# A diffusion block on one core: the first adaLN steps in another order, and some q products among them

## The chip, the cores and the metric

The kernel runs on one core of a Trainium2 chip. Its time is the device time of one execution in microseconds (us); lower is better. The time before is the median of three runs. A profile is one execution taken by the hardware profiler; all durations below come from that one. Engines are called PE (TensorE matmul), PEld (TensorE weight load), DVE (VectorE), ACT (ScalarE), POOL (GpSimd) and SP (SyncE, which here only issues DMAs).

## The reference, cut to what matters

One layer of a diffusion block: 256 latent tokens `x` and 256 context tokens `ctx`, width 2048. The part that the change touches is the start:

```python
sh1, sc1, g1, sh2, sc2, g2 = adaln(c, w_ada, b_ada)              # silu(c) @ w_ada + b_ada, in six
h  = modulate(rms_norm(x, norm_mix_g), sh1, sc1)                 # x * (1 + scale) + shift
csh1, csc1, ... = adaln(c_ctx, w_ada, b_ada)
hc = modulate(rms_norm(ctx, norm_mix_g), csh1, csc1)
q, k, v = split(h @ w_qkv, 3);  _, kc, vc = split(hc @ w_qkv, 3)  # 16 heads of 128
...                                                               # attention, w_o, gated residual
x = x + g2 * conv_ffn(modulate(rms_norm(x, norm_ffn_g), sh2, sc2), ...)
```

Keys and values are needed of both streams, queries of the latent one alone. Everything is float32.

## The kernel before

Features lie on partitions: the 2048 features of a token are 16 blocks of 128, called kt = 0 to 15. Tokens 0 to 255 are the latent stream (`xl`), 256 to 511 the context (`xc`). A float32 product is made of three products of halves: `hh` and `hl` are high and low part of the modulated input, `wh` and `wl` those of a weight, and L372, L373 and L374 multiply hh by wh, hh by wl and hl by wh. Each is a matmul of 512 columns for one tile of 128 tokens and one block kt. A weight is split by a cast on ACT (L157, `wh`) and a subtraction on DVE (L158, `wl`); the loaded tiles (`wr`) have four buffers, `wh` three, `wl` two.

The first stage goes by grains (L46): block 0, block 1, then seven pairs of blocks. Shift and scale of a grain come from an adaLN step (`ada_step`, L391): four loads of `w_ada` (tiles `wx`, four buffers, each loaded by two DMAs for shift and scale), sixteen small matmuls against the 32-column tile `s32` (L407), a copy to SBUF on ACT (`ev`, L414), transposes on PE (L417), and five small DVE operations that give `shT` and `gsT` (L422 to L430). `modulate` (L436) then makes a DVE product in place (L441), `hh` on ACT (L446) and `hl` on DVE (L447) for each block and stream.

Before the first products of a stream its rms must be known. `stats` (L349) squares the input on ACT in eight pieces (L354), adds them up on DVE (L359), sums over partitions by matmuls with one column (L229), takes the root (POOL L197, DVE L198 to L202), and spreads the result by a matmul (L220) and a copy (L222).

`first_products` (L455) gives the products of a grain in six pieces, each for two of the four tiles of 128 tokens (the first two are latent, the last two context): the first 512 columns of k, which gather in four PSUM banks over the whole stage (`pj`), and twice 512 columns of v, each grain of which goes through two banks (`mx`) and is copied (L472, ACT, first grain) or added (L474, DVE) to `vsum`. The two `mx` banks are also those of the sums and of the spread root in `stats`: they are given out in the order of the program, and each user waits until the one before has been read.

The program begins with `x`, its stats and adaLN step 0, the split of two weights (`ahead`, L182), the load of `ctx`, the latent pieces of k and of the first v of grain 0, the stats of `ctx`, and its modulation. Then a loop goes over the grains: the pieces of grain j stand between the four parts of step j+1. All loads of inputs and weights are issued by SP, in one queue. The order within an engine is set when the program is built, by a planner that simulates the instructions in time and goes by program order where several are ready; `tc.issue_after(i)` puts an instruction behind i on the same engine, and `tc.high_priority()` puts it ahead in the planner's choice. `plan` (L166) lists all weight tiles in the order of use.

After this stage `project(0, 2)` (L681) makes the first 512 columns of q from all 16 blocks: 2 token tiles, 16 blocks and 3 halves, 96 matmuls. Then come attention, the output projection, and the FFN, which takes over half of the time.

Of the kernel before, what the change touches and what calls it, by code (L numbers as in the profile page):

```python
# [15 lines left out]
P = 128  # L16
# [36 lines left out]
def block_kernel(  # L53
# [93 lines left out]
    last, hold = [], []  # L147

    def wpair(src, k0, kn, c0, cn):

        w = wload(src, k0, kn, c0, cn)
        hi = wp.tile([P, KT, CH], F32R, tag="wh", name="wh", bufs=3)
        lo = wp.tile([P, KT, CH], F32R, tag="wl", name="wl", bufs=2)
        with ExitStack() as order:
            for ins in hold:
                order.enter_context(tc.issue_after(ins))
            a = nc.scalar.copy(hi[:, :kn, :cn], w[:, :kn, :cn])  # L157
# [9 lines left out]
    for kt, n in GRAINS:  # L167
        plan.extend((w_qkv, kt, n, c, CH) for c in (D, 2 * D, 2 * D + CH))
    for g, cols in ((0, (0,)), (1, (D, 0)), (2, (2 * D, D, 0)), (3, (D, 0, 2 * D))):
        for c in cols:  # L170
            plan.extend((w_qkv, kt, KT, c + g * CH, CH) for kt in range(0, KD, KT))
    for pieces in WO:
# [175 lines left out]

    def stats(xin, name):  # L349

        sacc = None
        for kt in range(0, KD, 2):
            sq = xp.tile([P, 2, T], F32, tag="sq", name="sq", bufs=3)
            nc.scalar.activation(sq, xin[:, kt : kt + 2, :], AF.Square)  # L354
# [7 lines left out]
        return rstd_rows(xp, sums, name, nc.vector.tensor_copy)  # L362

    def nat(psl, tt0, w, kt0, n, first, last):

        wh, wl = w
        for i, pt in enumerate(psl):
            ts = slice((tt0 + i) * P, (tt0 + i + 1) * P)
            for k in range(n):
                kt = kt0 + k  # L370
                a, z = first and k == 0, last and k == n - 1
                nc.tensor.matmul(pt, hh[:, kt, ts], wh[:, k, :], start=a, stop=False)  # L372
                nc.tensor.matmul(pt, hh[:, kt, ts], wl[:, k, :], start=False, stop=False)  # L373
                nc.tensor.matmul(pt, hl(kt, ts), wh[:, k, :], start=False, stop=z)  # L374
            side.tick(side.rate)
            ada.tick(ada.rate)

    def project(c0, nt):
        psl = [pj() for _ in range(nt)]
        ada.rate = ADA_RATE[nt]  # L380
        for kt in range(0, KD, KT):
            nat(psl, 0, weight(w_qkv, kt, KT, c0, CH), kt, KT, kt == 0, kt == KD - KT)
        ada.rate = 0.0
        return psl
# [5 lines left out]

    def ada_step(b0, nb, work=()):  # L391

        ap_ = ms()
        n = 2 * nb * P
        for q in range(4):
            if q < len(work):
                work[q]()
            w = xp.tile([P, 4 * CH], F32, tag="wx", name="wx", bufs=4)[:, : 4 * n]
# [7 lines left out]
            for k in range(4):  # L406
                nc.tensor.matmul(  # L407
                    ap_[32 * k : 32 * k + 32, :n], s32[:, 4 * q + k, :], w[:, k * n : (k + 1) * n],
                    start=(q == 0), stop=(q == 3), tile_position=(0, 32 * k),
                )  # L410
        for piece in work[4:]:
            piece()
        ev = xp.tile([P, CH], F32, tag="ev", name="ev")
        nc.scalar.copy(ev[:, :n], ap_[:, :n])  # L414
        sp = ms()
# [4 lines left out]
        for which, dst in ((0, shT), (1, gsT)):  # L420
# [12 lines left out]
            op0=ALU.add, op1=ALU.mult,  # L433
        )

    def modulate(b0, nb, streams=None):  # L436

        for st, x_ in streams or ((0, xl), (1, xc)):
            t = slice(st * T, (st + 1) * T)
            for kt in range(b0, b0 + nb):  # L440
                nc.vector.scalar_tensor_tensor(  # L441
                    out=x_[:, kt, :], in0=x_[:, kt, :], scalar=gsT[:, kt, st : st + 1], in1=rb[st],
                    op0=ALU.mult, op1=ALU.mult,
                )
                sh = shT[:, kt, st : st + 1]
                nc.scalar.activation(hh[:, kt, t], x_[:, kt, :], AF.Identity, bias=sh)  # L446
                nc.vector.scalar_tensor_tensor(  # L447
                    out=hl(kt, t), in0=x_[:, kt, :], scalar=sh, in1=hh[:, kt, t].bitcast(F32),
                    op0=ALU.add, op1=ALU.subtract,
                )  # L450


    vsums = [kv.tile([P, 4, CH], F32, tag=tag, name="vsum") for tag in ("qq", "kl")]

    def first_products(b0, nb):  # L455

        st = {}
# [5 lines left out]

        def v_pair(g, h0):
            acc, c0 = vsums[g], 2 * D + g * CH
            if h0 == 0:
# [8 lines left out]

        return [
            lambda: k_pair(0), lambda: v_pair(0, 0), lambda: k_pair(2),
            lambda: v_pair(0, 2), lambda: v_pair(1, 0), lambda: v_pair(1, 2),
        ]
# [193 lines left out]

    def out_of_psum(pts, dst):

        for tt, pt in enumerate(pts):
            nc.scalar.copy(dst[:, tt, :], pt)
# [277 lines left out]
```

## Time and profile before

| | us |
|---|---|
| median of three runs (1419.31 to 1419.57) | 1419.35 |
| the profiled execution, its own time | 1419.36 |
| span of its instructions in the profile | 1417.6 |
| PE busy / DVE busy / ACT busy | 1386.8 / 1022.4 / 694.9 |
| first product of x (L372) starts | 23.72 |
| first product of ctx (L372) starts | 35.79 |
| moved by DMA | 317.13 MB |

In a timeline a row is: start in us, length in us, engine, line, operation, output and inputs with their shapes, how many were merged (x8), and in brackets the idle time of the engine before it and what ended that. In a table of windows a row is: the window, its length, then busy time and instructions of PE, PEld, DVE, ACT and POOL, the granted TensorE clock (1.00 is full), the busy share of the 16 DMA engines and the GB/s moved. In the chain of waits a row is start, length, and what the end of the program hung on then.

### The profile page before, as it was taken

Reading aid. Unit: us, or ns where it says so; the run is one execution under the profiler, and the core shown is the slowest. Engines: PE = TensorE matmul, PEld = TensorE weight load, DVE = VectorE, ACT = ScalarE, POOL = GpSimd, SP = SyncE. Lnnn points to the kernel's source line nnn. Section 1 sums busy time; section 2 is a strip of 40 time slices with the busy share of each in tenths; the row PEclk is TensorE's granted clock in tenths of the full one; section 3 lists DMA queues with packets and bytes.
Section 4 is the critical chain, followed back from the end, with each engine's and each line's share of the span. In section 5 each row is a group of like instructions: output and inputs, shape, how many; then the busy total and the mean of one; then the engine's idle time right before and its main releaser. Section 6 shows DMA issues by size and latency. Waiting matters only on the chain.

```text
span 1417.6 us, 20783 instructions
## 1 busy us (share of the span) xinstructions
PE 1386.8 (98%) x7608; PEld 1164.8 (82%) x7608; DVE 1022.4 (72%) x1669; ACT 694.9 (49%) x1212; POOL 59.9 (4%) x64
## 2 busy tenths in 40 slices
PE   4999999999999999999899999999999999999998
PEld 2566788888888888888788888888888888888888
DVE  4555678878877888788777888778787675545454
ACT  4322254564454564554565655556555554333343
POOL 1000010020010020000100000000000000000000
PEclk9999999999999999999899999999999999999999
DMA  9999637768776869475667777777776666666554
GB/s 304 357 353 292 223 104 237 227 214 257 233 238 192 276 201 291 157 250 178 225 187 237 237 236 238 225 237 235 231 230 189 175 192 197 188 200 201 169 181 154
DMA packets 208918, 317.13 MB, mean 224 GB/s; under 512 B 23360, under 2 KB 87744, under 8 KB 208816
## 3 DMA queue, kind: packets, MB, share of 16 engines
q1 hardware_dynamic: 208688, 315.79, 71.5%
q8 instruction: 59, 0.97, 0.3%
q14 instruction: 43, 0.35, 0.1%
q10 hardware_dynamic: 128, 0.01, 0.0%
HBM read 312.75 MB, written 3.01 MB: 223 GB/s over the span
## 4 chain that ended last, share of the span: by engine, by line
PE 94%; DMA 2%; DVE 2%; SPq 1%; ACT 1%; issue 1%; POOL 0%; DVEq 0%; ACTq 0%; POOLq 0%
PE pj L723 20%; PE pj L729 10%; PE mx L723 10%; PE pj L372 8%; PE pj L373 8%; PE pj L374 8%; PE ms L723 7%; PE mx L729 5%; PE ms L729 4%; PE mx L372 2%; PE mx L373 2%; PE ms L407 2%; PE mx L374 2%; DMA wx<-in_w_ada 1%; PE ms L627 1%; SPq L401 1%
## 5 line engine op out<-in xcount | busy, mean ns | idle before, releaser
L158 DVE TENSOR_TENSOR wl<-wr,wh 128x1024 fp32r<-128x1024 f32 (+2 forms) x425 | 478.1, 1126 | 284.8 <-PE pj L729 102.3
L157 ACT CAST wh<-wr 128x1024 fp32r<-128x1024 f32 (+2 forms) x425 | 412.6, 972 | 535.3 <-PE pj L723 164.3
L373 PE MATMUL pj<-wl,hh 128*128 128x512 f32 x512 | 202.7, 396 | 0.0
L374 PE MATMUL pj<-wh,hl 128*128 128x512 f32 x512 | 200.1, 393 | 0.0
L372 PE MATMUL pj<-wh,hh 128*128 128x512 f32 x512 | 193.0, 396 | 2.5 <-ACT hh L446 2.5
L274 DVE SCALAR_TENSOR_TENSOR acc<-wa,sT,acc 128x512 f32<-128x512 f32 x240 | 183.2, 765 | 2.5
L723 PE MATMUL pj<-hf,wh 128*128 128x512 f32 x688 | 176.1, 395 | 2.0 <-DVE hf L815 2.0
L723 PEld LDWEIGHTS pj<-hf,wh 128*128 128x128 f32 x688 | 124.6, 190 | 25.1 <-DVE hf L815 2.8
L372 PEld LDWEIGHTS pj<-wh,hh 128*128 128x128 f32 x512 | 95.7, 188 | 26.4 <-issue 3.4
L373 PEld LDWEIGHTS pj<-wl,hh 128*128 128x128 f32 x512 | 96.5, 188 | 21.5 <-DVE wl L158 0.9
L374 PEld LDWEIGHTS pj<-wh,hl 128*128 128x128 f32 x512 | 96.5, 188 | 18.8
L729 PEld LDWEIGHTS pj<-hf,wl 128*128 128x128 f32 x688 | 93.7, 190 | 6.7
L723 PE MATMUL mx<-hf,wh 128*128 128x512 f32 x352 | 97.7, 394 | 0.0
L729 PE MATMUL pj<-hf,wl 128*128 128x256 f32 x688 | 96.9, 283 | 0.0
L723 PE MATMUL ms<-hf,wh 128*128 128x512 f32 x336 | 90.9, 390 | 0.0
L723 PEld LDWEIGHTS ms<-hf,wh 128*128 128x128 f32 x336 | 63.1, 188 | 14.2
L474 DVE TENSOR_TENSOR vsum<-vsum,mx 128x512 f32<-128x512 f32 x64 | 43.1, 682 | 34.3 <-PE mx L374 34.1
L723 PEld LDWEIGHTS mx<-hf,wh 128*128 128x128 f32 x352 | 60.6, 190 | 7.8
L729 PEld LDWEIGHTS mx<-hf,wl 128*128 128x128 f32 x352 | 53.7, 189 | 6.8
L729 PE MATMUL mx<-hf,wl 128*128 128x256 f32 x352 | 55.9, 282 | 0.0
L729 PE MATMUL ms<-hf,wl 128*128 128x256 f32 x336 | 54.7, 283 | 0.0
L407 PE MATMUL ms<-wx,s 128*32 128x512 f32 (+1 forms) x288 | 36.9, 582 | 16.3 <-DMA wx<-in_w_ada 16.3
(248 smaller groups left out, 2029.6 us busy)
## 6 DMA issues: line engine op xcount, KB each, us to landing
wr<-in_w_up SPq DMA_DIRECT2D x160, 512.0 KB, 4.2
wa<-in_w_ada SPq DMA_DIRECT2D x128, 512.0 KB, 4.8
wr<-in_w_qkv SPq DMA_DIRECT2D x93, 512.0 KB, 4.2
wr<-in_w_down SPq DMA_DIRECT2D x63, 512.0 KB, 4.6
wx<-in_w_ada SPq DMA_DIRECT2D x56, 512.0 KB, 8.6
wr<-in_w_o SPq DMA_DIRECT2D x24, 512.0 KB, 5.0
wr<-in_w_down SPq DMA_DIRECT2D x45, 256.0 KB, 3.1
wr<-in_w_up SPq DMA_DIRECT2D x16, 384.0 KB, 3.4
```

What stands on the lines that cost most here:

```text
L157: a = nc.scalar.copy(hi[:, :kn, :cn], w[:, :kn, :cn])
L158: b = nc.vector.tensor_tensor(out=lo[:, :kn, :cn], in0=w[:, :kn, :cn], in1=hi[:, :kn, :cn].bitcast(F32), op=ALU.subtract,)
L274: nc.vector.scalar_tensor_tensor(out=acc, in0=w[:, k, :], scalar=s, in1=acc, op0=ALU.mult, op1=ALU.add)
L372: nc.tensor.matmul(pt, hh[:, kt, ts], wh[:, k, :], start=a, stop=False)
L373: nc.tensor.matmul(pt, hh[:, kt, ts], wl[:, k, :], start=False, stop=False)
L374: nc.tensor.matmul(pt, hl(kt, ts), wh[:, k, :], start=False, stop=z)
L401: load = nc.sync.dma_start(w.rearrange("p (k s f) -> p k s f", k=4, s=2)[:, :, which, :], w_ada[q * CH : (q + 1) * CH, c0 : c0 + n // 2].r ...
L407: nc.tensor.matmul(ap_[32 * k : 32 * k + 32, :n], s32[:, 4 * q + k, :], w[:, k * n : (k + 1) * n], start=(q == 0), stop=(q == 3), tile_pos ...
L474: nc.vector.tensor_add(acc[:, h0 + i, :], acc[:, h0 + i, :], pr_[i])
L627: nc.tensor.transpose(tp[:, kt * P : (kt + 1) * P], pr[:, kt * P : (kt + 1) * P], ident)
L723: nc.tensor.matmul(pts[b][:, : t1 - t0], wh[:, k, bs], mov(kt, slice(t0, t1)), start=(kt == 0 and t0 == 0), stop=False,)
L729: nc.tensor.matmul(pts[b][:, :T], wl[:, k, bs], mov(kt, slice(0, T)), start=False, stop=(kt == kn - 1),)
```

## The change

The start of the program, up to adaLN step 3, is put in another order; no product is added or left out.

- Weights of q for blocks 0 and 1 are loaded early (`Q_EARLY`), and their products are made with grains 0 and 1 in the `mx` banks and gathered in `qsum` (ACT copies for block 0, DVE additions for block 1). `project(0, 2)` starts at block 2, and `qsum` is added when its banks are read, on DVE in place of a copy on ACT.
- The latent modulation of block 0 stands ahead of the splits of the first two weights (`hold`). The squares of `ctx` stand behind it, and the split of the third weight behind the last of these squares.
- The last two pairs of squares are no longer added up on DVE: they go into the sums as four more parts, 12 matmuls of one column and not 8.
- The four parts of an adaLN step are loaded together, ahead of the pieces; for steps 0 and 1, which are half as wide, two parts share a `wx` buffer. Before the loop there stand the load of the third weight and those of step 1.
- `BEHIND` says, for steps 1 to 3, how many pieces of the grain before stand ahead of each part of the step. For step 1 it is (2, 2, 2, 2): all of its matmuls come behind the context pieces of k and of the first v, and the last two pieces (both of the second v) behind the matmuls. Their rest (`ada_end`) and their modulation get priority.

```diff
+Q_EARLY = 2
+
+BEHIND = {0: (2, 2, 2, 2), 1: (2, 2, 4, 5), 2: (2, 2, 4, 4)}
...
     for kt, n in GRAINS:
-        plan.extend((w_qkv, kt, n, c, CH) for c in (D, 2 * D, 2 * D + CH))
+        cs = (0,) * (kt == 0) + (D, 2 * D, 2 * D + CH) + (0,) * (0 < kt < Q_EARLY)
+        plan.extend((w_qkv, kt, n, c, CH) for c in cs)
...
-    def stats(xin, name):
+    def squares(xin, behind=()):
...
+                for ins in behind:
+                    order.enter_context(tc.issue_after(ins))
+                square = nc.scalar.activation(sq, xin[:, kt : kt + 2, :], AF.Square)
             if sacc is None:
                 sacc = sq
-            else:
+            elif kt < KD - 4:
                 nacc = xp.tile([P, 2, T], F32, tag="sacc", name="sacc", bufs=2)
                 nc.vector.tensor_add(nacc, sacc, sq)
                 sacc = nacc
-        sums = col_sums(mx()[:, 0:2], (sacc[:, 0], sacc[:, 1]))
+            else:
+                parts.extend((sq[:, 0], sq[:, 1]))
...
+    def ada_step(ws, b0, nb, work=(), behind=None):
         ap_ = ms()
         n = 2 * nb * P
+        done = 0
+        for q, w in enumerate(ws):
+            with ExitStack() as order:
+                for piece in work[done : behind[q] if behind else q + 1]:
+                    piece()
+                    done += 1
+                if behind:
+                    order.enter_context(tc.issue_after(last_mm[0]))
+                for k in range(4):
+                    mm = nc.tensor.matmul(
...
+        with ExitStack() as order:
+            if behind:
+                order.enter_context(tc.issue_after(mm.ins))
+            for piece in work[done:]:
+                piece()
+        with ExitStack() as order:
+            if behind or not work:
+                order.enter_context(tc.high_priority())
+            return ada_end(ap_, b0, nb)
...
+        q = [lambda: pair(qsum, 0, 0)]
+        pieces = [
             lambda: k_pair(0), lambda: v_pair(0, 0), lambda: k_pair(2),
             lambda: v_pair(0, 2), lambda: v_pair(1, 0), lambda: v_pair(1, 2),
         ]
+        return (q if b0 == 0 else []) + pieces + (q if 0 < b0 < Q_EARLY else [])
 
     stream(xl, xT)
-    rb = [stats(xl, "x")[0]]
-    ada_step(*GRAINS[0])
+    rb = [stats(squares(xl)[0], "x")[0]]
+    copied = ada_step(ada_load(*GRAINS[0]), *GRAINS[0])
+    with tc.high_priority():
+        x_ins = modulate(*GRAINS[0], ((0, xl),))
+    hold[:] = [copied, x_ins[0]]
     ahead()
+    hold.clear()
     stream(xc, ctxT)
-    modulate(*GRAINS[0], ((0, xl),))
+    loaded.append(wload(*plan[0]))
+    tiles = ada_load(*GRAINS[1])
+    parts, square = squares(xc, x_ins[-1:])
+    hold[:] = [square]
     work = first_products(*GRAINS[0])
-    work[0]()
-    work[1]()
-    rb.append(stats(xc, "c")[0])
-    modulate(*GRAINS[0], ((1, xc),))
+    for piece in work[:3]:
+        piece()
+    hold.clear()
+    with tc.high_priority():
+        rb.append(stats(parts, "c")[0])
+        modulate(*GRAINS[0], ((1, xc),))
     for j, grain in enumerate(GRAINS):
-        work = first_products(*grain) if j else work[2:]
+        work = first_products(*grain) if j else work[3:]
         if j + 1 < len(GRAINS):
-            ada_step(*GRAINS[j + 1], work)
-            modulate(*GRAINS[j + 1])
+            if j:
+                tiles = ada_load(*GRAINS[j + 1])
+            ada_step(tiles, *GRAINS[j + 1], work, BEHIND.get(j))
+            with ExitStack() as order:
+                if j in BEHIND:
+                    order.enter_context(tc.high_priority())
+                modulate(*GRAINS[j + 1])
...
-    q = split_q(out_of_psum(project(0, 2), qw))
+    q = split_q(out_of_psum(project(0, 2, Q_EARLY), qw, qsum))
```

More of the change, by code (lines that the diff above doesn't have):

```diff
@@ L360, in stats @@
                 sacc = nacc
-        sums = col_sums(mx()[:, 0:2], (sacc[:, 0], sacc[:, 1]))
-        return rstd_rows(xp, sums, name, nc.vector.tensor_copy)
+            else:
+                parts.extend((sq[:, 0], sq[:, 1]))
+        return (sacc[:, 0], sacc[:, 1], *parts), square.ins
+    def stats(parts, name):
+        return rstd_rows(xp, col_sums(mx()[:, 0:2], parts), name, nc.vector.tensor_copy)
+    last_mm = []
     def nat(psl, tt0, w, kt0, n, first, last):
@@ L373, in nat, with project @@
                 nc.tensor.matmul(pt, hh[:, kt, ts], wl[:, k, :], start=False, stop=False)
-                nc.tensor.matmul(pt, hl(kt, ts), wh[:, k, :], start=False, stop=z)
+                mm = nc.tensor.matmul(pt, hl(kt, ts), wh[:, k, :], start=False, stop=z)
+                last_mm[:] = [mm.ins]
             side.tick(side.rate)
             ada.tick(ada.rate)
-    def project(c0, nt):
+    def project(c0, nt, k_lo=0):
         psl = [pj() for _ in range(nt)]
         ada.rate = ADA_RATE[nt]
-        for kt in range(0, KD, KT):
-            nat(psl, 0, weight(w_qkv, kt, KT, c0, CH), kt, KT, kt == 0, kt == KD - KT)
+        for kt in range(k_lo, KD, KT):
+            nat(psl, 0, weight(w_qkv, kt, KT, c0, CH), kt, KT, kt == k_lo, kt == KD - KT)
         ada.rate = 0.0
@@ L405, in ada_step, with ada_end @@
             loads.append(load.ins)
[L406 to L412, printed above, removed]
+            ws.append(w)
+        return ws
+    def ada_step(ws, b0, nb, work=(), behind=None):
+        ap_ = ms()
+        n = 2 * nb * P
+        done = 0
[8 more added lines that the diff above has]
+                    mm = nc.tensor.matmul(
+                        ap_[32 * k : 32 * k + 32, :n], s32[:, 4 * q + k, :],
+                        w[:, k * n : (k + 1) * n], start=(q == 0), stop=(q == 3),
+                        tile_position=(0, 32 * k),
+                    )
+        with ExitStack() as order:
[7 more added lines that the diff above has]
+            return ada_end(ap_, b0, nb)
+    def ada_end(ap_, b0, nb):
+        n = 2 * nb * P
         ev = xp.tile([P, CH], F32, tag="ev", name="ev")
-        nc.scalar.copy(ev[:, :n], ap_[:, :n])
+        copied = nc.scalar.copy(ev[:, :n], ap_[:, :n])
         sp = ms()
```

42 lines of the change are left out of this document (26 added, 16 removed).

## The prediction, made before the changed kernel was run

> **What bounds the kernel now.** I read the page first, then a table of windows, then the timeline of the first 60 us. From the page the busy times and the first line of the chain, from the windows the stretch behind the first context product and the next 100 us:
>
> ```profile
> PE 1386.8 (98%) x7608; PEld 1164.8 (82%) x7608; DVE 1022.4 (72%) x1669; ACT 694.9 (49%) x1212; POOL 59.9 (4%) x64
> ...
> PE 94%; DMA 2%; DVE 2%; SPq 1%; ACT 1%; issue 1%; POOL 0%; DVEq 0%; ACTq 0%; POOLq 0%
> ...
> 35.79:54.00 18.21, 17.48 (x92) 10.38 (x95) 9.42 (x24) 8.57 (x14) 0.00 (x0) 1.00 1.08 356
> 60.00:160.00 100.00, 100.00 (x515) 62.48 (x514) 56.74 (x113) 26.57 (x40) 0.00 (x0) 1.00 0.93 305
> ```
>
> TensorE sets the end. From the first context product at 35.79 on it has no hole but 0.73 us up to 54, and none at all from 60 to 160. So the change is worth what it does to two things: the moment from which PE is closed, and the PE work that still lies behind that moment. Work that moves from the closed part into the open part is a gain by its length; work that moves the other way is a loss.
>
> The open part first, up to the first product of x:
>
> ```profile
> 18.25 1.08 PE L407 MATMUL ms<-wx,s 128*32 128x256 f32 x8 [0.54 <-DMA wx<-in_w_ada]
> 18.85 1.33 ACT L157 CAST wh<-wr 128x512 fp32r<-128x512 f32 x2 [6.60 <-DMA wr<-in_w_qkv]
> 20.09 0.36 ACT L414 COPY ev<-ms 128x256 f32<-128x256 f32 x1
> ...
> 22.64 0.63 ACT L354 ACTIVATE sq<-xc 128x512 f32<-128x512 f32 x1 [0.37 <-DMA xc<-in_ctxT]
> 23.17 0.49 ACT L446 ACTIVATE hh<-xl,shT 128x256 fp32r<-128x256 f32 x1
> 23.72 0.80 PE L372 MATMUL pj<-wh,hh 128*128 128x512 f32 x1 [2.46 <-ACT hh L446]
> 24.31 0.63 PE L373 MATMUL pj<-wl,hh 128*128 128x512 f32 x1
> 24.74 0.63 PE L372 MATMUL pj<-wh,hh 128*128 128x512 f32 x1
> ```
>
> Step 0 ends on PE at 19.33 with its last load; its copy waits for the casts until 20.09, and `hh` stands behind a square until 23.17. Two matmuls lie 0.43 us apart here. Then the context:
>
> ```profile
> 25.59 1.15 ACT L354 ACTIVATE sq<-xc 128x512 f32<-128x512 f32 x2 [0.30 <-DMA xc<-in_ctxT]
> ...
> 28.46 1.07 ACT L472 COPY vsum<-mx 128x512 f32<-128x512 f32 x2 [1.21 <-PE mx L374]
> 28.86 0.64 PE L407 MATMUL ms<-wx,s 128*32 128x256 f32 x8 [0.21 <-DMA wx<-in_w_ada]
> 29.43 1.05 PE L229 MATMUL mx<-ones,sacc 128*128 128x1 f32 x8
> ...
> 32.09 0.42 DVE L215 TENSOR_TENSOR cd<-ident,cr 128x256 f32<-128x256 f32 x1
> 32.48 0.64 PE L407 MATMUL ms<-wx,s 128*32 128x256 f32 x8 [1.16 <-DMA wx<-in_w_ada]
> 33.05 0.70 PE L220 MATMUL mx<-cd,ones 128*128 128x256 f32 x2
> 33.78 0.42 DVE L222 COPY cb<-mx 128x256 f32<-128x256 f32 x1 [1.27 <-PE mx L220]
> 34.26 0.64 PE L407 MATMUL ms<-wx,s 128*32 128x256 f32 x8 [0.51 <-DMA wx<-in_w_ada]
> 34.95 0.37 ACT L414 COPY ev<-ms 128x256 f32<-128x256 f32 x1 [5.42 <-PE ms L407]
> 35.22 0.51 ACT L446 ACTIVATE hh<-xc,shT 128x256 fp32r<-128x256 f32 x1
> 35.38 0.44 PE L417 MATMUL ms<-ident,ev 128*128 128x128 f32 x2 [0.48 <-ACT ev L414]
> 35.79 0.50 PE L372 MATMUL pj<-wh,hh 128*128 128x512 f32 x1
> 37.44 0.51 ACT L446 ACTIVATE hh<-xl,shT 128x256 fp32r<-128x256 f32 x1 [1.70 <-DVE xl L441]
> ```
>
> The last of `ctx` has been squared at 26.74, but the sums start only at 29.43: their bank is one of the two `mx` banks that v of grain 0 holds until ACT has copied it. The wait behind the sums is used: all of step 1, four parts and the transposes, runs in it and is over when the context starts. That is the part of the old order which the change gives up.
>
> **The change, part by part.** The prices of PE work in the closed part:
>
> ```profile
> 43.73 0.39 PE L374 MATMUL mx<-wh,hl 128*128 128x512 f32 x1
> 44.05 1.06 PE L407 MATMUL ms<-wx,s 128*32 128x512 f32 x8
> 45.04 0.50 PE L372 MATMUL mx<-wh,hh 128*128 128x512 f32 x1
> 45.38 0.39 PE L373 MATMUL mx<-wl,hh 128*128 128x512 f32 x1
> ...
> 53.72 1.06 PE L407 MATMUL ms<-wx,s 128*32 128x512 f32 x8 [0.73 <-DMA wx<-in_w_ada]
> ...
> 171.07 0.39 PE L373 MATMUL pj<-wl,hh 128*128 128x512 f32 x1
> 173.33 0.39 PE L374 MATMUL mx<-wh,hl 128*128 128x512 f32 x1
> ```
>
> The second of the last two rows is the tenth matmul after the first: 2.26 / 10 = 0.226 us each. A part of adaLN between products costs 0.1 us more on the way in (44.05 - 43.73 - 0.23) and 0.1 on the way out (45.38 - 45.04 - 0.23).
>
> 1. *q products.* 12 matmuls (2 blocks, 2 tiles, 3 halves) leave the closed stage of `project`: -2.71 us. The 6 of block 0 go into the open part. The 6 of block 1 need step 1 and stay closed: +1.36. Net **-1.36**.
> 2. *Step 1 behind the context.* Its matmuls can't fill the wait any more. Four parts at 0.57 (29.43 - 28.86), transposes 0.41 (35.79 - 35.38) and one way in and out 0.2 become closed work: **+2.9**.
> 3. *Start of the context.* Without casts ahead of the copy and squares ahead of `hh`, step 0's end at 19.33 gives `hh` by about 22.3 (20.09 to 23.17 is 3.08, less 0.7 behind the square; 19.35 + 2.4 + its own 0.5). Only then come the eight squares of `ctx`, 0.575 each: to 26.9, no earlier than now. On ACT follow two copies of q out of `mx` (1.07) and the cast of the first v (0.66), which now stands behind the squares: 28.6. The latent v products start between 28.0 and 28.6, take 6 x 0.226, are copied (0.53), and the sums start between 29.5 and 30.5; 12 matmuls instead of 8, at 0.13, end between 31.1 and 32.1. From there to the first context product it was 30.48 to 35.79, 5.3 us; two delays go: L220 waited 0.5 behind a part of step 1 (32.51 to 33.05), `hh` 0.5 behind `ev`. 4.3 remain: 35.4 to 36.4. So the shorter chain on DVE, the priority and the free queue of PE are eaten up by q's six matmuls and copies ahead of the bank. I take **0**, ends -0.4 and +0.6.
> 4. *Wait at 53.72.* Three groups of work now stand ahead of that part, so the load is there: **-0.73**.
> 5. *Parts taken together.* Step 2 in three groups for four, step 3 in two: 3 x 0.2, **-0.6**.
> 6. *Start of grains 1 and 2.* From the end of step 1's last part (34.90) to the end of `hh` (37.95) it takes 3.05. The second v of grain 0, 12 matmuls, and the transposes cover 3.1: nothing. For step 2 as many matmuls are left (a pair of v, a pair of q), but two blocks are to be modulated and vsum additions stand on DVE: **+0.5**, ends 0 and 1.3.
> 7. *The clock.* This stall shows elsewhere in this trace, ahead of the FFN, with its windows:
>
> ```profile
> 676.68 0.64 PE L729 MATMUL ms<-om,wl 128*128 128x256 f32 x4
> 679.09 1.68 PE L229 MATMUL ms<-ones,sq 128*128 128x1 f32 x8
> 683.12 1.19 PE L220 MATMUL mx<-yd,ones 128*128 128x256 f32 x2 [2.36 <-issue]
> 686.35 3.78 PE L723 MATMUL pj<-hf,wh 128*128 128x512 f32 x8 [2.03 <-DVE hf L815]
> ...
> 680.00:690.00 10.00, 5.61 (x15) 4.06 (x16) 7.38 (x17) 5.66 (x11) 3.21 (x4) 0.50 0.88 307
> 690.00:700.00 10.00, 10.00 (x60) 8.90 (x59) 9.97 (x17) 7.44 (x14) 3.42 (x5) 1.00 0.31 83
> ```
>
> There the same sums and spread stand alone on PE between dense products. Under 3 us after the last of these the granted clock is 0.50, and it is whole again only at 690, 3.7 us after 686.35. The old start escapes that: step 1's parts lie in its wait, and the pace at 171 is already reached at 28.86. With step 1 pinned behind the context, PE has from about 29.7 to 35.8 nothing but one-column matmuls and one spread. I expect the half clock there, and products at 0.43 instead of 0.226 for some 4 us (3.7 at the FFN; 23.72 to about 28 at the start): **+2.0**. Ends: 0 if the clock stays, 2.1 by the longer spell.
>
> The Trainium skill, "TensorE: Matmul & The Clock Gate", section "Part 1: The HAM clock gate", speaks against the change here: one idle window of some 3.4 us halves the clock, one busy window restores it, and the windows run free. By that rule the slow spell would be 3.4 to 6.8 us long and cost 1.7 to 3.4 (an estimate), and the sum would be 2.4 to 4.1. The FFN rows agree with it.
>
> At nothing I cost: two half casts and subtractions for each whole one, and two additions for copies of q at L677 (DVE 72%, ACT 49% busy); the two early loads on SP, 0.74 us each at 356 GB/s (after 53.72 no part waits for a load, and 305 GB/s from 60 to 160 shows room). Were that cover gone, each would cost its 0.6 to 1.5 us.
>
> Sum: 2.9 - 1.36 + 0 - 0.73 - 0.6 + 0.5 = +0.7, and with the clock **+2.7 us**. The profiled execution took 1419.36 (span 1417.6 and 1.8 around it), the median 1419.35: 1422.1.
>
> **Rivals.**
>
> *The clock stays.* The sums and the spread keep PE awake, or the hole is shorter. For it: in the old wait PE was busy for only 4.5 of 7.1 us (four parts, sums, spread, transposes), and kept its pace. Against: the FFN rows. +0.7: 1420.1.
>
> *The context starts early.* If the banks are free when the squares end, 26.9 + 1.6 + 4.3 = 32.8: 3.0 earlier, the hole is too short for the clock, and the sum is -2.3: 1417.1; without the stall of item 6, 1416.5. Against: the order of `mx` banks in the program. It passes 0.2% (2.8 us, about what a measurement can tell from no change) if the context starts by 32.3.
>
> *Weights behind a blocked load (slower still).* The third load of step 2 goes into a buffer of step 1, which is now read after the context, near 40; SP issues in order. If the first v weight of grain 1 stands behind the third and fourth load, it lands after another 6 us of transfers and the way, near 50; it is wanted near 47.5. +2.5 on top: 1424.6. It decides if that weight is issued behind step 1's parts. For it: the loads stand first in the program. Against: the planner can take a load that is ready ahead of one that isn't, as it did before.
>
> *The change doesn't do what it says:* the planner gives nearly the old order, and only q counts, 1418.0. Against: the new edges bind. It shares the rest with small shifts later.
>
> **How the numbers follow.** Forecast 0.42 (own range 1421.2 to 1423.5), clock stays 0.22, early context 0.17, blocked weights 0.12, rest 0.07. Slower by over 0.2% (above 1422.2): half of the forecast, the blocked weights, half of the rest, 0.37. Faster by over 0.2% (below 1416.5): two thirds of the early context and the rest's other half, 0.14. Within: 0.49. The range goes from the early context to the blocked weights, 1416.2 to 1425.0.
>
> **What would show it.** Right: first product of x near 22.5, of the context between 35.4 and 36.4; in between no L407; a granted clock of 0.50 in a window around 34 to 38, and context products 0.43 us apart; step 1 in one block after 12 products; no wait at step 3. Wrong: a context product before 33.5, a clock of 1.00 throughout, or a PE wait for `wr` or `wl` between 45 and 52.

## The result, and the profile after

| | before | after |
|---|---|---|
| median, us (4 runs each) | 1419.33 (1417.37 to 1419.57) | 1436.18 (1435.10 to 1437.94) |
| ratio, with its 95% interval | | 1.0118 (1.0103 to 1.0133) |
| profiled execution / its span, us | 1419.36 / 1417.6 | 1436.98 / 1435.2 |

The changed kernel is 16.85 us slower, not 2.7, and well above the 1425.0 at which the range ended. The page of after: its busy times, the first line of its chain, and a group of products (busy time, mean ns, then idle time ahead of them):

```profile
PE 1400.2 (98%) x7640; PEld 1176.6 (82%) x7640; DVE 1019.7 (71%) x1670; ACT 695.5 (48%) x1213; POOL 64.2 (4%) x64
...
PE 95%; DVE 3%; DMA 1%; issue 0%; ACT 0%; POOL 0%; SPq 0%; DVEq 0%; ACTq 0%
...
L392 PE MATMUL pj<-wh,hh 128*128 128x512 f32 x508 | 194.4, 401 | 4.7 <-ACT hh L499 4.7
```

PE is busy for 13.4 us more, though no product of a weight was added (the 32 records more are those of the longer sums). Busy time grows where a matmul runs at half clock or an adaLN part is cut up. DVE takes a percent more of the chain, and `hh` a wait that it did not have. Line numbers have moved: L392 to L394 are the products (L372 to L374 before), L446 adaLN (L407), L237 the sums (L229), L228 the spread (L220), L499 `hh` (L446).

First the start, from the timeline of after:

```profile
13.56 3.55 PE L237 MATMUL mx<-ones,sq 128*128 128x1 f32 x16
...
23.48 0.51 ACT L499 ACTIVATE hh<-xl,shT 128x256 fp32r<-128x256 f32 x1 [1.33 <-DVE xl L494]
...
29.96 0.99 PE L392 MATMUL mx<-wh,hh 128*128 128x512 f32 x2 [0.43 <-ACT wh L163]
31.46 1.07 ACT L529 COPY vsum<-mx 128x512 f32<-128x512 f32 x2 [1.06 <-PE mx L394]
32.10 1.05 PE L237 MATMUL mx<-ones,sacc 128*128 128x1 f32 x8 [0.22 <-ACT vsum L529]
33.01 1.93 PE L237 MATMUL mx<-ones,sq 128*128 128x1 f32 x16
37.10 1.19 PE L228 MATMUL mx<-cd,ones 128*128 128x256 f32 x2 [2.17 <-DVE cd L223]
39.31 0.51 ACT L499 ACTIVATE hh<-xc,shT 128x256 fp32r<-128x256 f32 x1 [4.58 <-DVE xc L494]
39.87 0.79 PE L392 MATMUL pj<-wh,hh 128*128 128x512 f32 x1 [1.58 <-ACT hh L499]
40.47 0.63 PE L393 MATMUL pj<-wl,hh 128*128 128x512 f32 x1
...
43.44 0.62 PE L394 MATMUL pj<-wh,hl 128*128 128x512 f32 x2
```

The reader is to see three things. The sums are 8 and 16 records where before had 8 alone: they stand ahead of step 0, so `hh` of x comes at 23.48 and not at 22.3. The context starts at 39.87, 4.1 us after before's 35.79. And it starts at half pace, 0.42 from one product to the next: eight of them take 3.57 to 43.44, where 8 x 0.23 would be 1.8. Then, from the same timeline, step 1, and the start of grain 2 (blocks 2 and 3) with the longer pieces of work of DVE between the transposes of its step and its `hh`:

```profile
44.45 1.93 PE L446 MATMUL ms<-wx,s 128*32 128x256 f32 x32
...
62.91 0.60 PE L468 MATMUL ms<-ident,ev 128*128 128x128 f32 x4
63.02 1.22 DVE L164 TENSOR_TENSOR wl<-wr,wh 128x1024 fp32r<-128x1024 f32 x1
64.15 0.68 DVE L531 TENSOR_TENSOR vsum<-vsum,mx 128x512 f32<-128x512 f32 x1
64.89 0.50 PE L392 MATMUL mx<-wh,hh 128*128 128x512 f32 x1 [0.68 <-DVE vsum L531]
64.92 0.68 DVE L531 TENSOR_TENSOR qsum<-qsum,mx 128x512 f32<-128x512 f32 x1
65.71 1.22 DVE L164 TENSOR_TENSOR wl<-wr,wh 128x1024 fp32r<-128x1024 f32 x1
66.93 0.68 DVE L531 TENSOR_TENSOR qsum<-qsum,mx 128x512 f32<-128x512 f32 x1
67.53 0.87 DVE L494 SCALAR_TENSOR_TENSOR xl<-xl,gsT,xb 128x256 f32<-128x256 f32 x2
68.60 0.80 PE L392 MATMUL pj<-wh,hh 128*128 128x512 f32 x1 [2.74 <-ACT hh L499]
...
73.89 0.51 PE L394 MATMUL pj<-wh,hl 128*128 128x512 f32 x1
```

Step 1 is one block behind twelve context products, as forecast. Between the transposes at 62.91 and the modulation at 67.53 two weight splits (1.22 each), one `vsum` and two `qsum` additions (0.68 each) stand in DVE's queue among the small operations of `ada_end`. PE runs dry twice, 0.68 and 2.74, and comes back at half pace: twelve products in the 5.29 to 73.89, 2.5 more than at the full pace of 0.23. The table of windows of after shows both spells (the granted clock is the third number from the end):

```profile
37.00:43.00 6.00, 4.32 (x9) 2.99 (x10) 2.09 (x4) 0.51 (x1) 0.00 (x0) 0.50 0.63 216
...
68.00:74.00 6.00, 5.40 (x13) 4.25 (x14) 2.77 (x8) 1.71 (x4) 0.00 (x0) 0.50 0.98 334
```

A third loss lies later. These are the adaLN groups of step 5, which the change does not pin, from the timeline of PE in after:

```profile
108.24 2.77 PE L446 MATMUL ms<-wx,s 128*32 128x512 f32 x20
...
112.52 1.90 PE L446 MATMUL ms<-wx,s 128*32 128x512 f32 x10
...
115.96 1.05 PE L446 MATMUL ms<-wx,s 128*32 128x512 f32 x2
```

An adaLN matmul is two records (16 of them are x32), so a whole part of four is x8 and takes 1.06 (the rows at 44.05 and 53.72 of before). The single matmul at 115.96 takes 1.05 as well: the four of a part share their time only when they are issued together. The 32 records of this step take 5.72 against 4 x 1.06 = 4.24. Counted from each adaLN matmul to the next matmul of PE, steps 2 and 3 cost 0.4 less than before, and steps 5 and 6 3.3 more; over steps 2 to 8 it is 31.1 for 28.4.

The last place is far from the edit. These are windows of after: from the start of `project` to the output projection, that projection (products with `om`), and the FFN's products (those with `hf`):

```profile
210.60:590.40 379.80, 377.93 (x1852) 315.21 (x1851) 318.52 (x539) 192.88 (x428) 47.52 (x35) 1.00 0.75 232
590.40:694.40 104.00, 102.06 (x627) 90.27 (x628) 81.87 (x140) 54.55 (x93) 0.00 (x0) 1.00 0.57 185
702.90:1189.30 486.40, 486.35 (x2773) 427.94 (x2774) 378.69 (x597) 280.57 (x441) 5.88 (x7) 0.99 0.71 217
```

And the first two of them for before:

```profile
193.50:576.70 383.20, 382.47 (x1877) 319.20 (x1876) 320.46 (x542) 196.22 (x433) 43.10 (x35) 1.00 0.75 232
576.70:677.00 100.30, 99.33 (x613) 88.67 (x614) 79.11 (x136) 53.65 (x91) 0.00 (x0) 1.00 0.57 189
```

Fourteen matmul records of the last attention group stand behind the first `om` product in after that stood ahead of it before, and PE's idle time in the two stages is 1.87 + 1.94 against 0.73 + 0.97. Both stages together take 483.8 us; 483.5 less the 2.7 of q would be 480.8. That is 3.0 lost.

The account, in us: context start +4.1; step 1 in the closed part +2.2 (1.86 and ways in and out, transposes 0.15); q of block 1 +1.4; half clock at the context +1.7 (8 products at 0.43); second wait +3.4 and its slow spell +2.5; adaLN parts of steps 2 to 8 +2.7; the wait at 53.72 of before -0.7. That is 17.3, and `project` starts 17.1 later (210.6 for 193.5); a wait of 0.38 at 50.01 is not in it. Then -2.7 for q, +3.0, and about +0.2 around the start of the FFN: 17.6, the difference of the spans.

### The profile page after: what moved, and what is told of

The parts are those of the page before. It is cut to its first block, busy times and chain, and to the rows that moved or that the text cites. A ratio compares the mean times of both kernels' runs of the same rounds, so it can differ in the third digit from the quotient of the medians.

```text
span 1435.2 us, 20835 instructions
## 1 busy us (share of the span) xinstructions
PE 1400.2 (98%) x7640; PEld 1176.6 (82%) x7640; DVE 1019.7 (71%) x1670; ACT 695.5 (48%) x1213; POOL 64.2 (4%) x64
## 3 DMA queue, kind: packets, MB, share of 16 engines
q1 hardware_dynamic: 208704, 315.79, 70.8%
## 4 chain that ended last, share of the span: by engine, by line
PE 95%; DVE 3%; DMA 1%; issue 0%; ACT 0%; POOL 0%; SPq 0%; DVEq 0%; ACTq 0%
PE pj L803 20%; PE pj L809 10%; PE mx L803 9%; PE pj L392 8%; PE pj L393 8%; PE pj L394 8%; PE ms L803 7%; PE mx L809 5%; PE ms L809 4%; PE ms L446 3%; PE mx L392 2%; PE mx L393 2%; PE mx L394 2%; PE ms L704 1%; DVE wl L164 1%; PE mx L237 1%
## 5 line engine op out<-in xcount | busy, mean ns | idle before, releaser
L392 PE MATMUL pj<-wh,hh 128*128 128x512 f32 x508 | 194.4, 401 | 4.7 <-ACT hh L499 4.7
L394 PE MATMUL pj<-wh,hl 128*128 128x512 f32 x508 | 198.2, 394 | 0.0
L392 PEld LDWEIGHTS pj<-wh,hh 128*128 128x128 f32 x508 | 96.1, 190 | 29.0 <-ACT hh L499 6.3
L394 PEld LDWEIGHTS pj<-wh,hl 128*128 128x128 f32 x508 | 96.1, 189 | 19.9 <-issue 0.8
L392 PE MATMUL mx<-wh,hh 128*128 128x512 f32 x132 | 55.5, 422 | 2.9 <-ACT hh L499 1.8
```

What stands on the lines that cost most here:

```text
L394: mm = nc.tensor.matmul(pt, hl(kt, ts), wh[:, k, :], start=False, stop=z)
```

## The experiments

All were compared with before on the same chip, whose medians were 1419.84 to 1420.90. "Less than after" is against the 1436.18 above.

**Taking parts of the change back.** First all pins away:

```diff
-BEHIND = {0: (2, 2, 2, 2), 1: (2, 2, 4, 5), 2: (2, 2, 4, 4)}
+BEHIND = {}
```

> The changed kernel without BEHIND: the parts of steps 1 to 3 stand between the pieces again, and their rest and modulation have no priority; all else as changed. Theory (the loss is PE time lost at two places, the wait for the context and the wait at 64 to 69 us before grain 2, each with a spell of half clock behind it): step 1 goes back into the first wait (-2.2 us), the second wait and its slow spell go (-6), but step 1's parts now stand ahead of the context's sums in PE's queue and wait for their load until about 33, so the context starts no earlier: near 1429. Rival (the loss is in q's early products and the sums of twelve matmuls, the pins do little): within 2 us of 1436.

1429.45 (1.0068, 1.0053 to 1.0083), 6.7 less than after. Then the pins of steps 2 and 3 alone away, `BEHIND = {0: (2, 2, 2, 2)}`:

> The changed kernel with BEHIND for step 1 alone; steps 2 and 3 stand between the pieces as before. Theory: the start up to 50 us stays as changed; the wait of 3.4 us before grain 2 and the slow spell after it (2.7) go: near 1430. Rival (the second wait comes from the late start, not from the order of step 2): the wait stays and the time is near 1436.

1429.30 (1.0065, 1.0049 to 1.0082), 6.9 less. The second wait (3.4) and its slow spell (2.5) are gone, the parts of steps 2 to 8 cost 27.9 for 31.1, the context starts 1.6 earlier (38.24; nothing ahead of it is edited, so this is a difference between two executions); against that two waits for adaLN weights (0.42 and 1.48) are new. So `project` starts at 201.8, 8.8 earlier, of which the output projection gives back 1.9 (105.9, with half clock from 582.8 to 586.1). By this run the pins of steps 2 and 3 are the dearest part of the change. The pin of step 1 makes no difference between these two kernels: without it, the sums stand behind adaLN parts that wait for loads, and the context starts at 42.93.

The two pairs of squares added on DVE again, 4 matmuls for 12:

```diff
-            elif kt < KD - 4:
+            else:
...
-            else:
-
-                parts.extend((sq[:, 0], sq[:, 1]))
```

> The changed kernel with all eight squares added up on DVE again, so that the sums are 4 matmuls (8 instructions) and not 12 (24). Theory: the sums of the context take 1.0 and not 2.9 us, the context starts 1.9 earlier or, with step 0 no longer behind the sums of x, up to 3 earlier; the slow spells stay: 1433 to 1434.5. Rival (the parts save DVE time and the chain on DVE ends last): no gain or 1 us slower.

1434.00 (1.0099, 1.0084 to 1.0114), 2.2 less; x starts at 22.90, the context at 36.30, 3.6 earlier than in after. Not all of this is the edit's: with the long sums in place the context started at 38.24 in the run above and at 38.62 in the run with the credit below, so 1.9 to 2.3 is left for it. The second wait is as long as in after (2.75 of idle time for 2.74).

No early q: the plan, the pieces and `project(0, 2)` as before.

```diff
-            k_lo = 0 if c + g else Q_EARLY
+            k_lo = 0
...
-        return (q if b0 == 0 else []) + pieces + (q if 0 < b0 < Q_EARLY else [])
+        return pieces
...
-    q = split_q(out_of_psum(project(0, 2, Q_EARLY), qw, qsum))
+    q = split_q(out_of_psum(project(0, 2), qw))
```

> The changed kernel without the early products of q: all 16 blocks of q are made in project as before. Theory: six half-rate products (2.6 us) and two copies (1.1 us) leave the chain to the context, which starts 2 to 3.5 us earlier; 1.4 us of closed work come back net of block 1's products, and DVE has two qsum additions less before grain 2 (1.4 us less wait): 1432 to 1434. Rival (early q pays, as forecast): near 1437.5, slower by the 1.4 us.

1430.76 (1.0078, 1.0063 to 1.0093), 5.4 less, more than was expected. The second wait did not get shorter: 2.99 for 0.68 and 2.74. With two `qsum` additions and a split less in DVE's queue the first product of grain 2 comes 3.6 us behind the transposes and not 5.7, but PE has six products less to fill that time. The output projection is back at 100.3. That pointed to the pacing: `project` adds a fixed credit (0.1) for each token tile of each pair of blocks, by which the later adaLN work (gates and the FFN's modulation) is dealt out, and with one pair fewer `project(0, 2)` hands out 0.2 less.

```diff
+    ada.credit += 0.2
     q = split_q(out_of_psum(project(0, 2, Q_EARLY), qw, qsum))
```

> The changed kernel, and ada.credit raised by 0.2 ahead of project(0, 2): the two ticks of 0.1 that its two missing token tiles of block 0 and 1 no longer give. Nothing else differs. Theory (the output projection takes 104.1 us and not 100.3 since the shorter project hands on the later adaLN work at other moments, and with it the last group of attention): back to 100.3, 1432.4. Rival (the additions of qsum on DVE, or the planner for some other reason): stays at 104, near 1436.

1431.38 (1.0082, 1.0067 to 1.0097), 4.8 less. Nothing at the start is touched. The same two windows of this kernel:

```profile
209.10:589.20 380.10, 379.65 (x1865) 316.99 (x1864) 320.56 (x543) 193.70 (x429) 42.01 (x35) 1.00 0.76 232
589.20:689.50 100.30, 99.35 (x613) 88.71 (x614) 79.38 (x136) 54.16 (x92) 0.00 (x0) 1.00 0.58 190
```

The 613 records and the 100.3 us of before are back, 480.4 for both stages. Early q costs here through a budget that someone else reads. The profiled executions of after and of this kernel differ by 5.9, and not all of that is the credit's. In the two stages lie 3.4. Another 1.5 lies ahead of `project` (209.1 for 210.6), where the two kernels are the same: the context starts at 38.62, and the clock is back at 1.00 by 70.8 where after has it back at 74.1. The last 1.1 is in the FFN's products (486.4 for 485.3), fewer of which ran at half clock.

**Doing one part alone in the old kernel.** Step 1 behind the context, nothing else:

```diff
+        if pin:
+            work[0]()
+            work[1]()
...
+            with ExitStack() as order:
+                if pin:
+                    order.enter_context(tc.issue_after(last_mm[0]))
...
+            for piece in work[2 if pin else 4 :]:
```

> The kernel before with one thing of the change: the four parts of step 1 behind the context pieces of k and of the first v, the second v behind them. Theory (the wait for the context is open time that step 1 used, and its parts kept the clock up): the context starts at about 35, the granted clock halves ahead of it, 2.9 us of step 1 become closed work: 1422 to 1425. Rival (PE's queue is cleared and the context starts 1 us earlier, that decides): 1418 to 1419.5.

1427.66 (1.0056, 1.0039 to 1.0073): 7.5 slower than before, 2.7 above the upper end expected. A window of this kernel (the last two numbers are the share of the DMA engines and GB/s) and its timeline say why:

```profile
34.00:40.00 6.00, 4.92 (x22) 3.59 (x26) 1.83 (x4) 1.33 (x3) 0.00 (x0) 0.64 0.14 33
```

Timeline of the same kernel, SP's queue among it:

```profile
39.53 1.93 PE L416 MATMUL ms<-wx,s 128*32 128x256 f32 x32
...
40.23 8.59 SPq L407 DMA_DIRECT2D wx<-in_w_ada  x8
...
47.48 1.07 PE L416 MATMUL ms<-wx,s 128*32 128x512 f32 x8 [2.80 <-DMA wx<-in_w_ada]
```

The DMA engines stand at 0.14 while step 2's loads wait for the buffers of step 1; they go out from 40.23, just behind step 1's start, and PE waits 2.8 for one, with a second spell at half clock behind it, and 1.93 for `hh` of the next grain at 65.96. This is the mechanism of the third rival, with a `wx` load late in place of a weight. After shows no such wait; its shared buffers and earlier loads are the likely reason, which was not tried alone.

Early q alone in the old kernel, by the q lines of the change:

```diff
-            plan.extend((w_qkv, kt, KT, c + g * CH, CH) for kt in range(0, KD, KT))
+            k_lo = 0 if c + g else 2
+            plan.extend((w_qkv, kt, KT, c + g * CH, CH) for kt in range(k_lo, KD, KT))
...
+        return (q if b0 == 0 else []) + pieces + (q if b0 == 1 else [])
...
-    q = split_q(out_of_psum(project(0, 2), qw))
+    q = split_q(out_of_psum(project(0, 2, 2), qw, qsum))
```

> The kernel before with the early products of q alone: block 0 ahead of the latent k and v pieces, block 1 behind the other pieces of grain 1, project from block 2, qsum. Theory (q stands in the mx banks and in PE's and ACT's queue ahead of the sums): the context starts 3 to 4 us later, 1.4 us of closed work are saved net, and the output projection takes 104 us for 100.3: 1424 to 1426. Rival (as forecast, it pays): 1417 to 1418.

1427.43 (1.0046, 1.0031 to 1.0060): 7.3 slower, 1.4 above the upper end expected. From its timeline:

```profile
31.36 1.05 PE L231 MATMUL mx<-ones,sacc 128*128 128x1 f32 x8
...
37.99 0.80 PE L374 MATMUL pj<-wh,hh 128*128 128x512 f32 x1 [1.85 <-ACT hh L448]
38.58 0.63 PE L375 MATMUL pj<-wl,hh 128*128 128x512 f32 x1
```

The q products and their copies stand ahead of the sums (31.36 for 29.43 before), the context starts 2.2 later (3 to 4 were expected) and at half pace, and the output projection takes 104.1 as in after. Early q alone loses far more than the 2.7 it takes out of `project`.

**The three suspects together, and what is left.** Pins of steps 2 and 3 away, short sums and the credit restored:

```diff
-BEHIND = {0: (2, 2, 2, 2), 1: (2, 2, 4, 5), 2: (2, 2, 4, 4)}
+BEHIND = {0: (2, 2, 2, 2)}
...
-            elif kt < KD - 4:
+            else:
...
+    ada.credit += 0.2
```

> The changed kernel with three things undone together: BEHIND for step 1 alone, all squares added on DVE (4 matmuls in the sums), and the credit of 0.2. What is left of the change is early q, step 1 behind the context, and the new order of splits and loads. If the three losses are apart from each other (6.9, 2.2 and 3.7 to 4.8 us as run alone), they add up: 1422.5 to 1423.5. Rival (they share one cause, the late start): 1426 or more.

1423.05 (1.0022, 1.0013 to 1.0031), 13.1 less than after. The three one by one gave 6.9 + 2.2 + 4.8 = 13.9, so they about add up. As part of the 6.9 and of the 4.8 came from a start that those two edits do not touch, the closeness is in part luck.

Then the edits of the first, third and fourth run together:

```diff
+BEHIND = {}
...
+            else:
...
+    q = split_q(out_of_psum(project(0, 2), qw))
```

> The changed kernel without BEHIND, without early q and with all squares added on DVE: what is left is the modulation of x ahead of the first splits, the squares and the third split behind it, the four loads of a step together and two parts in one buffer. Theory (these cost nothing and win a little: x starts 1 us earlier, step 1's parts lie in the wait again and keep the clock up): 1418.5 to 1420.5, the same as before. Rival (the loads of a step ahead of the weights, or the split passes of adaLN, cost something by themselves): 1422 or more.

1421.39 (1.0005, 0.9996 to 1.0014), 0.9 above the upper end expected: what is left is the modulation ahead of the casts, the holds, the joined loads and the shared buffers. No difference to before can be measured. x starts at 22.29, earlier by 1.4, but the context at 36.99, later by 1.2, and at half pace:

```profile
36.99 0.79 PE L389 MATMUL pj<-wh,hh 128*128 128x512 f32 x1 [1.26 <-ACT hh L496]
37.58 0.63 PE L390 MATMUL pj<-wl,hh 128*128 128x512 f32 x1
```

That is a miss: the four parts of step 1 lie in the wait again (the last at 33.13), and did not keep the clock up. The same holds for early q alone in the old kernel. And the kernel of the last experiment below, whose start is that of before, has a clock of 0.50 from 31.1 to 34.4 in this wait, and only happens to be whole again when its context starts, at 35.53. That before shows no slow spell here was in part luck.

**The clock.** Products that nobody reads were put into the wait for the context, so that PE stays busy; in the changed kernel first:

```diff
+            with tc.issue_after(after or sums_mm[0]):
+                for _ in range(14):
+                    mm = nc.tensor.matmul(
+                        d[:, :T], hh[:, 0, 0:P], hh[:, 0, 0:T], start=True, stop=True,
+                    )
```

> The changed kernel with 28 products more, whose results nobody reads: 14 of 256 columns between the sums of the context and the spread of its root, 14 between the spread and the context's first product, where PE waits. It is work added. Theory (the clock falls in this wait because PE has nothing but one-column matmuls there): the granted clock stays at 1.00 through the wait, the context products lie 0.23 us apart, 1.7 us are won there and up to 0.7 at the spread: near 1434, although PE does 3 us more. Rival (the half rate has another cause, or costs nothing because the work behind it waits anyway): 1436 or more.

1436.59 (1.0115, 1.0099 to 1.0132): no better than after, where 1434 was expected. A window of its profile:

```profile
28.00:34.00 6.00, 5.32 (x18) 4.31 (x18) 0.74 (x2) 2.90 (x6) 0.00 (x0) 0.51 1.13 316
```

Two rows of its timeline, then the row of after that matches the first of them:

```profile
23.15 0.73 PE L418 MATMUL mx<-wh,hh 128*128 128x512 f32 x2 [1.78 <-ACT hh L525]
...
28.68 1.28 PE L418 MATMUL mx<-wh,hh 128*128 128x512 f32 x2 [2.52 <-ACT wh L163]
```

```profile
24.04 1.22 PE L392 MATMUL mx<-wh,hh 128*128 128x512 f32 x2 [1.78 <-ACT hh L499]
```

The clock was at half before the fill began, so this run does not say what a fill is worth. The instructions up to there are the same as in after, but their pace is not: the first products of x lie 0.23 us apart here and 0.43 in after. They end at 26.2 and not at 29.5, PE then waits 2.52 us for the cast of the third weight (0.43 in after, at 29.96), and goes on at half pace. The fill ran at half pace too and held the context back to 42.82, which then ran at full pace. (The table of windows gives 1.00 for after from 24 to 28 us, where its products lie 0.43 apart; so early in the profile the spacing has to be read, and not that column.) The same with 16 in the kernel that has the three suspects undone:

```diff
-                for _ in range(14):
+                for _ in range(16):
```

> three_undone with 32 products more that nobody reads, 16 between the sums of the context and the spread, 16 behind the spread. The sums are short here, so the clock should still be whole when the first of them start, which it was not with warm_ctx. Theory (as at the FFN, the half rate of the first 3.6 us of context products is lost time): the granted clock stays at 1.00 from the latent products on, the context products lie 0.23 us apart: 1.8 us won there and up to 0.5 at the spread, 1420.8 to 1421.5. Rival (what is won there is waited for later, at the loads of step 2, since PE waited 1.9 us for one at 50): 1422.5 to 1423.5.

1417.80 (0.9978, 0.9969 to 0.9987): faster than before, 5.2 less than without the fill, and 3.0 below the lower end expected. The spread and the first context products, from the timeline without the fill and then with it:

```profile
33.26 1.19 PE L228 MATMUL mx<-cd,ones 128*128 128x256 f32 x2 [2.17 <-DVE cd L223]
36.03 0.80 PE L389 MATMUL pj<-wh,hh 128*128 128x512 f32 x1 [1.58 <-ACT hh L496]
36.63 0.63 PE L390 MATMUL pj<-wl,hh 128*128 128x512 f32 x1
```

```profile
32.95 0.67 PE L235 MATMUL mx<-cd,ones 128*128 128x256 f32 x2 [0.15 <-DVE cd L227]
35.37 0.40 PE L415 MATMUL pj<-wh,hh 128*128 128x512 f32 x1
35.60 0.40 PE L416 MATMUL pj<-wl,hh 128*128 128x512 f32 x1
```

The start of the context (0.7, of which 0.3 is there already at the first product of x) and eight products at 0.23 for 0.43 (1.6) explain 2.3 of the 5.2. Behind them PE waits 1.5 for 2.9 in all, and the parts of steps 2 to 8 cost 27.1 for 28.0. The order of the two kernels differs there, so how much of this the fill did is open.

Last, the same fill in the old kernel's wait ahead of the FFN, where the prediction had read the slow spell: 8 products ahead of the sums, 18 behind them and 18 behind the spread.

```diff
+    spare, seen = pj(), split[0][1][0]
...
+        with tc.issue_after(after):
+            for _ in range(n):
+                mm = nc.tensor.matmul(
+                    spare[:, :T], seen[:, 0, 0:P], seen[:, 0, 0:T], start=True, stop=True,
+                )
...
+    fill(8, last_proj[0])
```

> The kernel before with 44 products more, whose results nobody reads, in the wait ahead of the FFN: 8 between the last product and the sums, 18 between the sums and the spread, 18 behind the spread, each of 256 columns on a weight tile that lies there. Theory (after a wait with one-column matmuls alone PE runs at half rate for 3.7 us, and that is lost time): the granted clock stays at 1.00 or is back before the FFN's first product, which starts no later; the eight first products take 2.0 and not 3.8 us: 1.5 to 2 us faster than before, near 1417.7. Rival (the first products wait for hf anyway): no change.

1416.03 (0.9967, 0.9954 to 0.9979): faster than before (1420.12 beside it) with nothing else changed, and by more than the 1.5 to 2 us expected. In its timeline, where before had the spread at 683.12 (1.19) and the first products at 686.35 (3.78):

```profile
682.32 0.67 PE L225 MATMUL mx<-yd,ones 128*128 128x256 f32 x2
682.63 2.50 PE L803 MATMUL pj<-wh 128*128 128x256 f32 x18
685.02 2.11 PE L733 MATMUL pj<-hf,wh 128*128 128x512 f32 x8
```

1.3 from the earlier start and 1.7 from the pace: 3.0 of the 3.2 by which the two profiled executions differ (1419.36 and 1416.17).

## Why the prediction was wrong

*What bounds the kernel* held: PE sets the end, and work pinned behind the context start is lost to the open part. *Item 2* (step 1, +2.9) measured 2.2: the four parts in one block take 1.86, where I had 0.57 for each, and the transposes 0.15 for 0.41. *Item 4* held too.

*Item 3*, the context start at no change, is the first step that failed: +4.1. I read "x8" as eight matmuls and wrote "12 matmuls instead of 8", as the list of the change does; it was 4 matmuls of two records, and became 12 of 24 records. Set against the code, which sums two halves for two tiles of tokens, the eight records would have shown it. Against the latest start that I gave, 36.4, the sums begin 1.6 late (32.10 for 30.5), take 1.3 longer (2.8 for 1.6), and from their end to the first product 4.9 passes for 4.3, as the half clock that I had priced for the products also slowed the spread (1.19 for 0.70). The 1.3 is the misread count. The 1.6 comes from a late x (24.04 where 22.5 was forecast), behind the longer sums of x and a step 0 at half pace, and it was not there in other executions with the same start: with the pins of steps 2 and 3 away, and with the credit, the sums begin at 30.46 and 30.70.

*Item 6*, the start of grains 1 and 2 (+0.5, at most 1.3), is the largest: 3.4 of idle time, and 2.5 at half clock behind it. I had counted what PE has left to do, and named the two modulations and the `vsum` additions on DVE, without adding the queue up: two splits, three additions and the reductions are 4.6 us from 62.91 to 67.53. The pins put the parts of step 2 behind the pieces that would have filled that time: without the pins of steps 2 and 3 the wait is gone. The length of the slow spell varies: 6.8 us in after, 3.4 us in the run with the credit, behind the same wait.

*Item 7* had the size right: clock 0.50, context products 0.43 apart, 1.7 lost where 2.0 stood. Its reason, that step 1's parts keep the clock up in the old start, did not hold: with them in the wait the clock fell as well in three other kernels, and whether the slow spell reaches the context products differed from one to the next. So the 1.7 can't be put down to the pin of step 1, and that the number fits is in part luck. In after itself the rival "the clock stays" is out. From the windows of the Trainium skill, "TensorE: Matmul & The Clock Gate", "Part 1: The HAM clock gate", I had estimated 1.7 to 3.4 for one such spell; the 1.7 and the 2.5 measured agree.

*Item 5*, parts together (-0.6), came out as +2.7. For the two steps that it spoke of it was nearly right, -0.4. What I left out is that the planner lays the later steps anew when the earlier ones move, and cut the four-matmul parts of steps 5 and 6 into pieces that each pay the full time. Steps 2 to 8 cost 31.1 with the pins of steps 2 and 3, also with the credit, with short sums or without early q; 27.9 without these two pins; and 32.6 without any pin, in part because step 2 then ran at half clock (5.7 for 3.9). What makes the planner cut was not tried. The sum should have had some 3 us for it in its range.

*Item 1*, q at -1.36, was right as far as its matmuls go, and wrong as a whole: what it adds ahead of the sums and the 0.2 of adaLN credit cost more than it saves. The credit stood nowhere in my sum: 3.0 by the windows of before and after, 3.4 by those of the run that restores it.

*The rivals.* "Weights behind a blocked load" did not happen here but did where step 1 alone was pinned, with a wait near the price foreseen (2.5 forecast, 2.8 measured). "The context starts early" was the wrong way round. "The change doesn't do what it says" is out: step 1 stands in one block behind twelve context products. All rivals kept to one stall and one slow spell. The kernel had two of each, and a stall of 2.7 us cost the spell behind it as well.

## What to carry to other kernels

Before a queue is emptied of work, write down what that work did besides: fill a wait, or spend a pacing credit that others read. For every pinned step, add up the whole queue of the engine that prepares the next products (here DVE), not only of the engine that waits. A wait of 2.7 us on TensorE was paid twice here, and unread products in a wait can pay: 1416.03 against 1420.12 with nothing else changed. One profile that shows a whole clock is no promise for the next.

## What the runs showed of the hardware

- A matmul of plain float32 operands (sums, spread, adaLN) stands in the records as two: 4 sums are x8, 12 are x24. A product of fp32r halves is one.
- Four 32-column matmuls (512 columns moving, full clock) issued together take 1.06, one alone 1.05.
- The pace does not follow from the program alone: the first products of x lie 0.43 apart in after and 0.23 in the kernel with the 28 unread products, behind the same instructions. The page of the Trainium skill named above says in the same part that the windows run free; these two rows agree.
- Every change of the clock in these traces lies a whole multiple of 3.41 us behind the one before. The half clock held for 3.41, 6.83, 10.24 or 13.65 us.
- The length of a wait alone does not say whether the clock falls. Ahead of the output projection PE waited 2.05 us with the pins of steps 2 and 3 away, and a spell of 3.4 us at half clock followed; with the 28 unread products it waited 2.46 there, and the clock stayed at 1.00. In the first 75 us, single waits of 2.52 to 2.99 between products all had half clock behind them (six kernels), those of 1.48 to 1.93 none (four kernels).

Whether the fill ahead of the FFN and the one ahead of the context add up was not tried.
